# Attention scores: the second passes of the two maps on 64 rows each, in one encoder-layer kernel

## The chip, the cores and the metric

The kernel runs on one core of a Trainium2 chip. The metric is the device time of one execution in microseconds, the median of several runs. A core has a matrix engine (TensorE; in the profile PE for its matmuls, PEld for the loads of its stationary operand), VectorE (DVE), ScalarE (ACT), GpSimd (POOL) and SyncE (SP), which here only issues DMAs. TensorE reads two operands from on-chip memory (SBUF): a stationary one, loaded into the array first, whose partitions are the rows of the array and the dimension that is summed over, and a moving one, which streams through column by column. It writes to PSUM, which has eight banks of 512 fp32 columns.

## The reference, cut to what matters

One layer of an encoder works on 1,024 prompt frames and 64 frames of a running stream, model width 1,024. Beside a gated linear recurrence and a feed-forward part it has differential attention with 8 heads: each head has two score maps of width 64, and its weights are the difference of two softmaxes.

```python
def _diff_attend(q, k, v, lam, mask):
    """q [B,Q,H,2,d], k [B,S,H,2,d], v [B,S,H,2d], mask [Q,S] -> [B,Q,H,2d]."""
    s = jnp.einsum('bqhcd,bshcd->bhcqs', q.astype(jnp.float32), k.astype(jnp.float32)) * DA_SCALE
    s = jnp.where(mask, s, -jnp.inf)
    p = jax.nn.softmax(s, axis=-1)
    w = p[:, :, 0] - lam * p[:, :, 1]
    return jnp.einsum('bhqs,bshe->bqhe', w.astype(v.dtype), v)
```

For the prompt the mask is causal in chunks of 64 frames, so query tile i (128 frames, i from 0 to 7) looks at the first 128(i+1) keys. All of it is fp32.

## The kernel before

The stages follow one another: the recurrence with its projections, head by head; attention, head by head; the branch projections, normalisation, the up projection with a convolution, the down projection. Attention runs from about 640 to 1,345 us of the execution.

**fp32 out of fp32r.** A wide fp32 operand is split into a high part, rounded to the matmul type fp32r, and a low part, the remainder. A projection (`proj_chunk`, L178) sums three products in PSUM: high by high, high by low, low by high.

**The scores.** The scores use the array's 128 rows for two products at once, as a map is only 64 wide. For a head and 512 keys, tile `B` holds for map m on that map's own 64 rows (map 0 on rows 0 to 63, map 1 on 64 to 127) the high part of k, and on the other 64 rows the low part of k, which a DMA moves there. Tile `A` holds for 256 queries, two passes and two maps the part of q: pass 0 the high part, pass 1 the low part, made on the map's own 64 rows (VectorE L588, GpSimd L589) and copied by a DMA on SP's queue to the other 64 rows (L590). So pass 0 gives q-high by k-high plus q-high by k-low, pass 1 gives q-low by k-high plus q-low by k-low, both on 128 rows.

**A head's attention** (`da_attend`) goes through the query tiles from 7 down to 0. For tiles 7 to 4 (over 512 keys) each map has a PSUM tile `s` of two banks; for tiles 3 to 0 both maps share one such tile, a bank each. The pool has two of them. Per map: the score matmuls (L641), a masking write (L649 or L658), the row maximum (VectorE, L650 or L659), the exponential (ScalarE, L652 or L662), after which the buffer is free. Then the maps are combined on VectorE (L669), transposed on TensorE (L676), copied (ScalarE, L677) and multiplied with the values (L682). Tile 7's scores of the next head stand between the transposes of its values (`nat`, L330); `ckt` (L611), `yt` (L538) and `wtd` (L720) are other transposes; `wtd`, and `yt` once a head, are on 64 rows.

**What sets the order.** The program is written head by head; a scheduler with a simulated timeline then orders each engine's instructions when the program is built. It puts matmuls of the projections (L178) of the next head and of the gates between the steps of a head's attention. On the chip each engine works in that order.

Of the kernel before, what the change touches and what calls it, by code (L numbers as in the profile page):

```python
# [10 lines left out]
F32 = mybir.dt.float32  # L11
# [9 lines left out]
P = 128  # L21
# [29 lines left out]
class K:  # L51
# [489 lines left out]
    def da_prep(self, h, mm, dp):  # L541
        nc, a, o = self.nc, self.a, self.o
        w = a["w_in"][0]
        c = h * P
        V, S, G = nc.vector, nc.scalar, nc.gpsimd

        def ev(dst, scale=None):
            def f(c0, cw, ps):
                if scale is None:
                    S.copy(dst[:, c0:c0 + cw], ps)  # L550
                else:
                    S.mul(dst[:, c0:c0 + cw], ps, scale)
            return f

        def st(name, shape=(P, T)):
            return dp.tile(list(shape), F32, tag="st", name=f"{name}{h}", bufs=3)

        kT = st("kT")
        self.proj(mm, self.wcols(w, 5120 + c), self.x, ev(kT))
        B = []  # L560
        for hf in range(2):
            b = dp.tile([P, 2, 512], F32R, tag="B", name=self.nm("B"), bufs=4)
            kl = dp.tile([P, 512], F32R, tag="KL", name=self.nm("KL"), bufs=1)
            sl = slice(hf * 512, hf * 512 + 512)
            for m in range(2):
                r = slice(m * 64, m * 64 + 64)
                V.tensor_copy(b[r, m, :], kT[r, sl])  # L567
                G.tensor_tensor(kl[r], kT[r, sl], b[r, m, :].bitcast(F32), ALU.subtract)  # L568
                ro = slice(64 - m * 64, 128 - m * 64)
                nc.sync.dma_start(b[ro, m, :].bitcast(F32), kl[r].bitcast(F32))  # L570
            B.append(b)
        kd2 = dp.tile([P, 2, 64], F32R, tag="kd2", name=f"kd2{h}", bufs=2)
        V.tensor_copy(kd2[:, 0, :], kT[:, TP:])
        V.tensor_tensor(kd2[:, 1, :], kT[:, TP:], kd2[:, 0, :].bitcast(F32), ALU.subtract)
        kn = st("kn", (P, 9, P))
        self.to_natural(mm, kT, kn, "mm")
        nc.sync.dma_start(o["k_prompt"][0, 0, :, h, :].rearrange("(c p) e -> p c e", p=P), kn[:, 0:8, :])
        nc.sync.dma_start(o["k_sample"][0, 0, :, h, :], kn[:64, 8, :])
        qT = st("qT")
        self.proj(mm, self.wcols(w, 4096 + c), self.x, ev(qT, 0.125))  # L580
        A = [None] * 4
        for hf in (3, 2, 1, 0):
            t = dp.tile([P, 2, 2, 256], F32R, tag="A", name=self.nm("A"), bufs=5)
            sl = slice(hf * 256, hf * 256 + 256)
            for m in range(2):
                r = slice(m * 64, m * 64 + 64)
                ro = slice(64 - m * 64, 128 - m * 64)
                V.tensor_copy(t[r, 0, m, :], qT[r, sl])  # L588
                G.tensor_tensor(t[r, 1, m, :], qT[r, sl], t[r, 0, m, :].bitcast(F32), ALU.subtract)  # L589
                nc.sync.dma_start(t[ro, :, m, :].bitcast(F32), t[r, :, m, :].bitcast(F32))  # L590
            A[hf] = t
        qb = self.qbd[h % 2]
        for m in range(2):
            r = slice(m * 64, m * 64 + 64)
            V.tensor_copy(qb[r, 0, r], qT[r, TP:])
            V.tensor_tensor(qb[r, 1, r], qT[r, TP:], qb[r, 0, r].bitcast(F32), ALU.subtract)
        vT = st("vT")
        self.proj(mm, self.wcols(w, 6144 + c), self.x, ev(vT))
        vn = dp.tile([P, 9, P], F32, tag="vn", name=f"dvn{h}", bufs=2)
        self.to_natural(mm, vT, vn, "mm")  # L600
        nc.sync.dma_start(o["v_prompt"][0, 0, :, h, :].rearrange("(c p) e -> p c e", p=P), vn[:, 0:8, :])
        nc.sync.dma_start(o["v_sample"][0, 0, :, h, :], vn[:64, 8, :])
        ck = dp.tile([P, 8, P], F32, tag="ck", name=f"ck{h}", bufs=1)
        nc.sync.dma_start(ck, a["cache_k"][0, 0, :, h, :].rearrange("(c p) e -> p c e", p=P))
        cv = dp.tile([P, 8, P], F32, tag="cv", name=f"cv{h}", bufs=1)
        nc.sync.dma_start(cv, a["cache_v"][0, 0, :, h, :].rearrange("(c p) e -> p c e", p=P))
        kd = []
        for g in range(2):
            ps = mm.tile([P, 512], F32, tag="mm", name=self.nm("ckt"))
            for j in range(4):  # L610
                nc.tensor.transpose(ps[:, j * P:(j + 1) * P], ck[:, g * 4 + j, :], self.ident)  # L611
            t = dp.tile([P, 2, 512], F32R, tag="kd", name=self.nm("kd"), bufs=2)
            S.copy(t[:, 0, :], ps)
            V.tensor_tensor(t[:, 1, :], ps, t[:, 0, :].bitcast(F32), ALU.subtract)
            kd.append(t)
        kd.append(kd2)
        return A, B, vn, cv, kd, qb

    def da_attend(self, h, prep, sc, xs, avp, dp):
        nc, o = self.nc, self.o  # L620
        c = h * P
        V, S, G = nc.vector, nc.scalar, nc.gpsimd
        A, B, vn, cv, kd, qb = prep
# [5 lines left out]
        for i in range(7, -1, -1):  # L629
            n = (i + 1) * P  # L630
# [3 lines left out]
            s = dp.tile([P, 6], F32, tag="sm", name=self.nm("sm"), bufs=4)  # L634
            qc = slice((i % 2) * P, (i % 2) * P + P)

            def scores(dst, m):
                for kc in range((n + 511) // 512):
                    kw = min(512, n - kc * 512)
                    for p in range(2):  # L640
                        nc.tensor.matmul(dst[:, kc * 512:kc * 512 + kw], A[i // 2][:, p, m, qc],  # L641
                                         B[kc][:, m, :kw], start=(p == 0), stop=(p == 1))

            if n > 512:
                E = []
                for m in range(2):
                    ps = sc.tile([P, 1024], F32, tag="sc", name=self.nm("s"))
                    scores(ps, m)
                    V.memset(ps[0:64, n - 64:n], NEG)  # L649
                    V.tensor_reduce(s[:, m:m + 1], ps[:, :n], AX.X, ALU.max, negate=True)  # L650
                    e = dp.tile([P, 1024], F32, tag="E", name=self.nm("E"), bufs=4)
                    S.activation(e[:, :n], ps[:, :n], AF.Exp, bias=s[:, m:m + 1], accum_out=s[:, 2 + m:3 + m])  # L652
                    E.append(e[:, :n])
            else:
                ps = sc.tile([P, 2, 512], F32, tag="sc", name=self.nm("s"))
                for m in range(2):
                    scores(ps[:, m, :], m)
                V.memset(ps[0:64, :, n - 64:n], NEG)  # L658
                V.tensor_reduce(s[:, 0:2], ps[:, :, :n], AX.X, ALU.max, negate=True)  # L659
                e = dp.tile([P, 2, 512], F32, tag="E", name=self.nm("E"), bufs=4)  # L660
                for m in range(2):
                    S.activation(e[:, m, :n], ps[:, m, :n], AF.Exp, bias=s[:, m:m + 1],  # L662
                                 accum_out=s[:, 2 + m:3 + m])
                E = [e[:, 0, :n], e[:, 1, :n]]
# [6 lines left out]
            for g in range((i + 4) // 4):  # L671
                nb = min(4, i + 1 - g * 4)
                ps = xs.tile([P, 512], F32, tag="x", name=self.nm("wt"))
# [4 lines left out]
            for kb in range(i + 1):  # L678
                with ExitStack() as es:
                    if self.last_av is not None:  # L680
                        es.enter_context(self.tc.issue_after(self.last_av.ins))
                    self.last_av = nc.tensor.matmul(av[:, i % n4, :], wT[:, kb, :], vn[:, kb, :],  # L682
                                                    start=(kb == 0), stop=(kb == i))
# [544 lines left out]
```

## Time and profile before

| | |
|---|---|
| median of 3 runs (lowest to highest) | 2390.39 us (2389.98 to 2395.66) |
| the profiled execution's own time | 2388.49 us |
| its span, first to last instruction | 2386.6 us |
| mean granted TensorE clock | 0.995 |
| TensorE matmuls busy | 2337.9 us, 98% of the span |
| VectorE, ScalarE, GpSimd busy | 65%, 46%, 22% |
| score matmuls (L641) | 384, mean 354 ns |

The profile comes from one execution. A matmul's length is modelled: matmuls overlap in the array, so the pace is read from one start to the next, not from the length. A row of the timeline gives start and length in microseconds, engine, line, operation, the tiles written and read, rows times columns of the array and the shape that streams, and a count where equal instructions were merged. In brackets stands idle time of the engine ahead of it, and what ended it.

### The profile page before, as it was taken

To read this page: it belongs to the slowest core of one execution; us is meant where nothing else is said; L and a number is where in the kernel's file an instruction comes from. 1 tells how busy PE (TensorE), PEld (TensorE's weight loads), DVE (VectorE), ACT (ScalarE), POOL (GpSimd) and SP (SyncE) were. 2 spreads that over 40 slices of the span, in tenths; PEclk is the share of its full clock that TensorE was granted. 3 is DMA by queue.
4 is the path that set the end of the run, shared out by engine and by line. 5 is a ranking of instruction groups with operands and counts; after the bars stand their busy time and mean duration, and the time that the engine had idled before them with its cause. 6 is when DMAs were issued, how large, how long until landed. Compare 5 with 4: busy or idle time off the path is not lost.

```text
span 2386.6 us, 42975 instructions
## 1 busy us (share of the span) xinstructions
PE 2337.9 (98%) x16534; PEld 2283.0 (96%) x16534; DVE 1540.2 (65%) x2682; ACT 1103.7 (46%) x2134; POOL 520.7 (22%) x576
## 2 busy tenths in 40 slices
PE   8999999999999999999999999999999999999997
PEld 8999999999999999999999999999999999989997
DVE  3666665555566565655657565488977877766764
ACT  3444444443344434434436543257444444466664
POOL 2222222222621121120120000022544444200100
PEclk9999999999999999999999999999999999999999
DMA  4111111112622332332336684444323223298865
GB/s 129 40 40 47 40 47 47 42 31 66 202 79 84 94 86 81 95 92 75 102 90 199 183 260 139 134 144 144 113 87 95 82 86 95 85 275 251 245 200 150
DMA packets 404580, 273.02 MB, mean 114 GB/s; under 512 B 21803, under 2 KB 393927, under 8 KB 404374
## 3 DMA queue, kind: packets, MB, share of 16 engines
q1 hardware_dynamic: 399638, 265.52, 37.5%
q10 hardware_dynamic: 4224, 4.46, 0.5%
q8 instruction: 130, 2.13, 0.4%
q0 software_dynamic: 512, 0.29, 0.1%
q14 instruction: 76, 0.62, 0.1%
HBM read 199.65 MB, written 57.96 MB: 108 GB/s over the span
## 4 chain that ended last, share of the span: by engine, by line
PE 89%; DMA 3%; DVE 3%; ACT 2%; issue 1%; POOL 0%; SPq 0%; POOLq 0%; DVEq 0%; ACTq 0%
PE mm L178 47%; PE mm L151 17%; PE mm L1166 9%; PE s L641 3%; PE av L682 2%; PE wt L676 1%; PE lv L404 1%; PE nat L330 1%; DMA gb<-s_g 1%; PE o L487 1%; DMA ydl<-s_yd 1%; DMA wraw<-w_down 1%; PE o L490 1%; PE avd L727 1%; DVE wlo L83 1%
## 5 line engine op out<-in xcount | busy, mean ns | idle before, releaser
L178 PE MATMUL mm<-x,whi 128*128 128x362 f32 (+1 forms) x3456 | 876.4, 333 | 5.2 <-DMA wraw<-w_in 2.2
L178 PEld LDWEIGHTS mm<-x,whi 128*128 128x128 f32 x3456 | 611.8, 189 | 11.0 <-ACT x L308 4.7
L178 PE MATMUL mm<-x,wlo 128*128 128x362 f32 (+1 forms) x1728 | 573.1, 332 | 0.0
L83 DVE TENSOR_TENSOR wlo<-wraw,whi 128x512 fp32r<-128x512 f32 x516 | 364.7, 712 | 263.6 <-ACT whi L82 257.1
L82 ACT CAST whi<-wraw 128x512 fp32r<-128x512 f32 x516 | 309.0, 605 | 429.8 <-PE mm L178 203.8
L178 PEld LDWEIGHTS mm<-x,wlo 128*128 128x128 f32 x1728 | 326.5, 189 | 1.7 <-issue 1.0
L1166 PE MATMUL mm<-ah,whi 128*128 128x288 f32 (+1 forms) x688 | 200.3, 292 | 2.1 <-ACT ah L1150 2.1
L1166 PE MATMUL mm<-al,whi 128*128 128x288 f32 (+1 forms) x688 | 199.9, 291 | 1.5 <-DVE al L1151 1.5
L1166 PE MATMUL mm<-ah,wlo 128*128 128x288 f32 (+1 forms) x688 | 200.1, 292 | 0.1
L1166 PEld LDWEIGHTS mm<-ah,whi 128*128 128x128 f32 x688 | 131.1, 191 | 2.7 <-ACT ah L1150 2.4
L1166 PEld LDWEIGHTS mm<-al,whi 128*128 128x128 f32 x688 | 130.8, 190 | 1.9 <-DVE al L1151 1.9
L1166 PEld LDWEIGHTS mm<-ah,wlo 128*128 128x128 f32 x688 | 130.6, 190 | 0.8 <-DVE wlo L83 0.8
L532 POOL TENSOR_TENSOR rs<-rs,mhalf 128x4 f32<-128x4 f32 (+1 forms) x24 | 22.0, 917 | 373.4 <-DVE rs L531 373.4
L568 POOL TENSOR_TENSOR KL<-kT,B 64x512 fp32r<-64x512 f32 x32 | 49.3, 1539 | 218.1 <-DVE B L567 193.5
L641 PE MATMUL s<-B,A 128*128 128x512 f32 (+3 forms) x384 | 87.8, 354 | 2.3 <-ACT E L662 1.6
L82 ACT CAST whi<-wsum 128x512 fp32r<-128x512 f32 x80 | 49.5, 620 | 87.4 <-PE mm L151 83.8
L165 DVE TENSOR_TENSOR u<-mm,p 128x272 f32<-128x272 f32 (+2 forms) x160 | 55.1, 366 | 49.5 <-PE mm L151 49.5
L384 POOL TENSOR_TENSOR P<-X,k 128x544 f32<-128x544 f32 (+1 forms) x32 | 60.3, 1884 | 122.8 <-ACT X L378 76.3
L677 ACT COPY wT<-wt 128x512 f32<-128x512 f32 (+1 forms) x96 | 46.3, 482 | 80.1 <-PE wt L676 79.5
L1081 DVE SCALAR_TENSOR_TENSOR c<-u,par,c 128x1090 f32<-128x1090 f32 x44 | 80.6, 1831 | 0.9 <-ACT c L1078 0.9
L682 PE MATMUL av<-dvn,wT 128*128 128x128 f32 x576 | 80.0, 275 | 0.5 <-ACT wT L677 0.5
L99 POOL TENSOR_TENSOR wsum<-wraw,wraw 128x512 f32<-128x512 f32 x40 | 70.4, 1760 | 43.7 <-DVE wlo L83 43.5
(382 smaller groups left out, 5882.2 us busy)
## 6 DMA issues: line engine op xcount, KB each, us to landing
wraw<-w_down SPq DMA_DIRECT2D x160, 256.0 KB, 3.6
wraw<-w_in SPq DMA_DIRECT2D x144, 256.0 KB, 2.9
wraw<-w_up SPq DMA_DIRECT2D x124, 256.0 KB, 3.1
wraw<-w_br_hg SPq DMA_DIRECT2D x48, 256.0 KB, 4.0
s_act<-c SPq DMA_DIRECT2D x22, 512.0 KB, 3.0
A<-A SPq DMA_DIRECT2D x64, 128.0 KB, 2.5
wraw<-w_out SPq DMA_DIRECT2D x32, 256.0 KB, 3.0
araw<-s_act SPq DMA_DIRECT2D x44, 144.0 KB, 4.0
```

Of the source, the lines that this page charges most:

```text
L82: nc.scalar.copy(hi[:, :kn, :], raw[:, :kn, :])
L83: nc.vector.tensor_tensor(lo[:, :kn, :], raw[:, :kn, :], hi[:, :kn, :].bitcast(F32), ALU.subtract)
L99: G.tensor_tensor(t, x, y, op)
L151: nc.tensor.matmul(ps, l, r, start=(first and k == 0 and i == 0), stop=(k == 3 and i == 2), skip_group_check=not first)
L165: V.tensor_tensor(dst, ps[:, sl], d[other][:, sl], ALU.add)
L178: nc.tensor.matmul(ps[:, :cw], l, r[:, :cw], start=(k == 0 and i == 0), stop=(k == n - 1 and i == 2))
L384: G.tensor_tensor(pk, xv[:, :, :hb], blocks(k, B)[:, :, :hb], ALU.mult)
L568: G.tensor_tensor(kl[r], kT[r, sl], b[r, m, :].bitcast(F32), ALU.subtract)
L641: nc.tensor.matmul(dst[:, kc * 512:kc * 512 + kw], A[i // 2][:, p, m, qc], B[kc][:, m, :kw], start=(p == 0), stop=(p == 1))
L682: self.last_av = nc.tensor.matmul(av[:, i % n4, :], wT[:, kb, :], vn[:, kb, :], start=(kb == 0), stop=(kb == i))
L1081: V.scalar_tensor_tensor(t[:, :W - 2], u[:, i, 1:W - 1], par[:, self.o_w1 + j:self.o_w1 + j + 1], t[:, :W - 2], ALU.mult, ALU.add)
L1166: nc.tensor.matmul(ps[:, :cw], l, r[f][:, :cw], start=(f == 0 and i == 0), stop=(f == NF - 1 and i == 2))
```

## The change

For query tiles 2 to 7 the second pass takes only the map's own 64 rows: q-low by k-high. The product q-low by k-low is left out there. Map 0's second pass stands on rows 0 to 63, map 1's on rows 64 to 127, and both write to different banks. Tiles 1 and 0 keep 128 rows. The loops are turned round: pass outermost, then the 512 keys, then the map, and for tiles 7 to 4 both maps' PSUM tiles are taken before the scores are written. Since the low part of q is no longer needed on the other 64 rows for queries from 256 on, those copies carry the high part alone (three of the four `A` tiles of a head).

```diff
@@ da_prep
-                nc.sync.dma_start(t[ro, :, m, :].bitcast(F32), t[r, :, m, :].bitcast(F32))
+
+                parts = slice(0, 1 if hf else 2)
+                nc.sync.dma_start(t[ro, parts, m, :].bitcast(F32), t[r, parts, m, :].bitcast(F32))
@@ da_attend
-            def scores(dst, m):
-                for kc in range((n + 511) // 512):
-                    kw = min(512, n - kc * 512)
-                    for p in range(2):
-                        nc.tensor.matmul(dst[:, kc * 512:kc * 512 + kw], A[i // 2][:, p, m, qc],
-                                         B[kc][:, m, :kw], start=(p == 0), stop=(p == 1))
+            def scores(dsts):
+
+
+                spans = [(kc, min(512, n - kc * 512)) for kc in range((n + 511) // 512)]
+                halves = [slice(0, P)] * 2 if i < 2 else [slice(0, 64), slice(64, P)]
+                for p in range(2):
+                    for kc, kw in spans:
+                        for m in range(2):
+                            r = halves[m] if p else slice(0, P)
+                            nc.tensor.matmul(dsts[m][:, kc * 512:kc * 512 + kw], A[i // 2][r, p, m, qc],
+                                             B[kc][r, m, :kw], start=(p == 0), stop=(p == 1))
 
             if n > 512:
                 E = []
-                for m in range(2):
-                    ps = sc.tile([P, 1024], F32, tag="sc", name=self.nm("s"))
-                    scores(ps, m)
+                pss = [sc.tile([P, 1024], F32, tag="sc", name=self.nm("s")) for _ in range(2)]
+                scores(pss)
+                for m, ps in enumerate(pss):
                     V.memset(ps[0:64, n - 64:n], NEG)
...
             else:
                 ps = sc.tile([P, 2, 512], F32, tag="sc", name=self.nm("s"))
-                for m in range(2):
-                    scores(ps[:, m, :], m)
+                scores([ps[:, m, :] for m in range(2)])
```

The scheduler makes a new order of it. Its rows name the tile written, the moving and the stationary one, and the tile written's shape. On TensorE, in head 4, query tile 7 stood like this before (`s_1237` is map 0, `s_1239` map 1, `B_1198` and `B_1200` the first and second 512 keys; x2 are the two passes):

```order
L330 MATMUL nat_1227_9236<-ident_67,vT4_9144 128x128 x4
L641 MATMUL s_1237_9277<-B_1198_8984,A_1214_9112 128x512 x2
L641 MATMUL s_1237_9277<-B_1200_8992,A_1214_9112 128x512 x2
L641 MATMUL s_1239_9286<-B_1198_8984,A_1214_9112 128x512 x2
L641 MATMUL s_1239_9286<-B_1200_8992,A_1214_9112 128x512 x2
L538 MATMUL yt_1138_8583<-ident_67,rt_1135_8572 128x128 x4
```

And now (`s_1237` map 0, `s_1238` map 1):

```order
L330 MATMUL nat_1227_9236<-ident_67,vT4_9144 128x128 x4
L648 MATMUL s_1237_9277<-B_1198_8984,A_1214_9112 128x512
L648 MATMUL s_1238_9278<-B_1198_8984,A_1214_9112 128x512
L648 MATMUL s_1237_9277<-B_1200_8992,A_1214_9112 128x512
L648 MATMUL s_1238_9278<-B_1200_8992,A_1214_9112 128x512
L648 MATMUL s_1237_9277<-B_1198_8984,A_1214_9112 128x512
L648 MATMUL s_1238_9278<-B_1198_8984,A_1214_9112 128x512
L648 MATMUL s_1237_9277<-B_1200_8992,A_1214_9112 128x512
L648 MATMUL s_1238_9278<-B_1200_8992,A_1214_9112 128x512
L538 MATMUL yt_1138_8583<-ident_67,rt_1135_8572 128x128 x4
```

The first four are the first passes on 128 rows, the last four the second passes, by turns on rows 0 to 63 and 64 to 127.

The next query tile, 6, before, map 0 (`s_1245`) and, after 18 projection matmuls, map 1 (`s_1247`):

```order
L676 MATMUL wt_1150_8633<-ident_67,E_1148_8625 128x128 x3
L641 MATMUL s_1245_9321<-B_1198_8984,A_1214_9112 128x512 x2
L641 MATMUL s_1245_9321<-B_1200_8992,A_1214_9112 128x384 x2
L178 MATMUL mm_1319_9647<-x00_96,whi_1314_9637 128x364
...
L676 MATMUL wt_1155_8657<-ident_67,E_1153_8649 128x128 x2
L641 MATMUL s_1247_9330<-B_1198_8984,A_1214_9112 128x512 x2
L641 MATMUL s_1247_9330<-B_1200_8992,A_1214_9112 128x384 x2
```

And now (map 0 `s_1245`, map 1 `s_1246`), with the same 18 between:

```order
L682 MATMUL wt_1150_8633<-ident_67,E_1148_8625 128x128 x3
L648 MATMUL s_1245_9321<-B_1198_8984,A_1214_9112 128x512
L648 MATMUL s_1245_9321<-B_1200_8992,A_1214_9112 128x384
L648 MATMUL s_1245_9321<-B_1198_8984,A_1214_9112 128x512
L648 MATMUL s_1245_9321<-B_1200_8992,A_1214_9112 128x384
L178 MATMUL mm_1319_9647<-x00_96,whi_1314_9637 128x364
...
L682 MATMUL wt_1155_8657<-ident_67,E_1153_8649 128x128 x2
L648 MATMUL s_1246_9322<-B_1198_8984,A_1214_9112 128x512
L648 MATMUL s_1246_9322<-B_1200_8992,A_1214_9112 128x384
L648 MATMUL s_1246_9322<-B_1198_8984,A_1214_9112 128x512
L648 MATMUL s_1246_9322<-B_1200_8992,A_1214_9112 128x384
```

Here each map's two second passes follow its own first passes, and the two maps' second passes do not stand next to each other.

## The prediction

> **What bounds the kernel now.** I read the page's busy shares and chain first, then one window over the attention stage, then what TensorE waits for in it.
>
> ```profile
> PE 2337.9 (98%) x16534; PEld 2283.0 (96%) x16534; DVE 1540.2 (65%) x2682; ACT 1103.7 (46%) x2134; POOL 520.7 (22%) x576
> PE 89%; DMA 3%; DVE 3%; ACT 2%; issue 1%; POOL 0%; SPq 0%; POOLq 0%; DVEq 0%; ACTq 0%
> 640.00:1345.00 705.00, 695.30 (x4484) 665.61 (x4482) 429.89 (x929) 322.16 (x730) 112.31 (x115) 1.00 0.36 104
> PE mm L178 <- ACT whi L82: 2.4, 2, 1.5
> PE s L641 <- ACT E L662: 1.6, 1, 1.6
> PE wt L676 <- ACT yT L539: 1.2, 5, 0.2
> PE wtd L723 <- ACT wTd L721: 1.0, 1, 1.0
> PE mm L178 <- DVE t L937: 0.8, 1, 0.8
> PE s L641 <- ACT E L652: 0.6, 1, 0.6
> PE ckt L611 <- ACT dvn L331: 0.6, 1, 0.6
> PE mm L178 <- DVE kd L614: 0.5, 1, 0.5
> PE av L682 <- ACT wT L677: 0.5, 1, 0.5
> ```
>
> TensorE is 98% busy, 89% of the chain lies on it, and in the 705 us of attention (granted clock 1.00) its waits sum to 9.2 us (the nine rows). VectorE has 275 us to spare there, ScalarE 383. So what the change does to TensorE's own stream is what it does to the time, nearly one for one; no other engine can take it up.
>
> **The pace of the stream.** In the next rows, of the timeline (start, length, engine, line), a wide matmul starts as fast as its columns pass: two of 362 columns from 1251.34 to 1251.67, 0.166 us each; which is 0.45 to 0.46 ns a column. Four score matmuls with 1,792 columns take 0.90 from 992.86 to 993.76, 0.81 by that pace and 0.09 at their first weight load. I take 0.231 us for 512 columns and 0.174 for 384. A weight load follows the one before it by 0.11 (a pair takes 0.30, one 0.19) and hides behind the running matmul.
>
> ```profile
> 992.86 1.06 PE L641 MATMUL s<-B,A 128*128 128x512 f32 x4
> 993.76 0.50 PE L178 MATMUL mm<-x,whi 128*128 128x364 f32 x2
> ...
> 1251.34 0.50 PE L178 MATMUL mm<-x,whi 128*128 128x362 f32 x2
> 1251.67 0.32 PE L178 MATMUL mm<-x,wlo 128*128 128x362 f32 x1
> ...
> 1252.17 0.32 PE L178 MATMUL mm<-x,wlo 128*128 128x362 f32 x1
> 1252.42 0.27 PE L538 MATMUL yt<-ident,rt 64*128 64x64 f32 x1
> 1252.63 0.60 PE L178 MATMUL mm<-x,whi 128*128 128x362 f32 x2
> 1253.06 0.33 PE L178 MATMUL mm<-x,wlo 128*128 128x362 f32 x1
> ```
>
> **What a matmul on 64 rows costs its neighbours.** The kernel has such matmuls already; L538 above is one, on 64 of the array's 128 rows (64*128) between two wide ones. The weight loads at the same place:
>
> ```profile
> 1252.01 0.19 PEld L178 LDWEIGHTS mm<-x,wlo 128*128 128x128 f32 x1
> 1252.42 0.14 PEld L538 LDWEIGHTS yt<-ident,rt 64*128 64x128 f32 x1 [0.23 <-PE mm L178]
> 1252.62 0.30 PEld L178 LDWEIGHTS mm<-x,whi 128*128 128x128 f32 x2
> ```
>
> The load for L538 isn't hidden any more: it starts 0.07 before the modelled end of the wide matmul (1252.49), and so does the load for the next wide one before L538's end (1252.69). After a 512-column matmul it is the same (end 799.53, load 799.45):
>
> ```profile
> 798.21 1.32 PE L641 MATMUL s<-B,A 128*128 128x512 f32 x5
> 799.45 0.14 PEld L538 LDWEIGHTS yt<-ident,rt 64*128 64x128 f32 x1 [0.36 <-issue]
> ```
>
> So where the row size changes, the array runs empty before weights go in. The next data come 0.11 after the load, 0.04 after the modelled end, where unchanged they would come at the pace: after 362 columns 0.32 + 0.04 against 0.166, 0.20 us lost; after the 512-column one, whose last started at 799.13 (798.21 + 4 x 0.231), 799.56 against 799.36, 0.20; by the mean modelled lengths of the score matmuls (408 and 338 ns, rows below) 0.22 after 512 columns and 0.20 after 384. **A change costs 0.20 us**, upper bound 0.22. Lower bound: the whole detour by L538, 1252.17 to 1253.06, 0.89, against 0.61 for the same four at their pace (3 x 0.166 + 0.11): 0.28 for two changes, 0.14 each, where a short matmul has little to hide anyway.
>
> The type isn't what costs: between score matmuls (fp32r) and plain fp32 ones on 128 rows nothing is lost. Three score matmuls from 1269.97 should take 2 x 0.231 + 0.12 = 0.58, and L682 starts 0.59 later:
>
> ```profile
> 1269.97 0.75 PE L641 MATMUL s<-B,A 128*128 128x512 f32 x3
> 1270.56 0.60 PE L682 MATMUL av<-dvn,wT 128*128 128x128 f32 x4
> ...
> L641 PE MATMUL s<-B,A 128*128 128x512 f32 x192 | 57.8, 408 | 0.7 <-ACT E L652 0.6
> L641 PE MATMUL s<-B,A 128*128 128x384 f32 x64 | 15.1, 338 | 0.0
> ```
>
> **The change, part by part.** *Row-size changes added.* By the order of the changed program, only query tiles 7, 3 and 2 issue both maps' second passes next to each other. In tiles 6, 5 and 4 all of map 0 comes first, both passes, then projection matmuls, then all of map 1, since map 1's PSUM buffer is freed later. So a head has 1 + 3 x 2 + 1 + 1 = 9 excursions to 64 rows, 18 changes; eight heads make 144. A count over TensorE's whole order gives 252 changes of row size against 100 (in a few heads another matmul splits an excursion in two): **152 more, x 0.20 = 30.4 us** (21 at 0.14, 33 at 0.22).
>
> *Time saved.* A 64-row matmul streams as many columns as a 128-row one, so it saves only where its partner runs at once: two pairs of 512 in tile 7, one of 512 in tile 3, one of 384 in tile 2; 32 pairs of the 80. No row here shows two at once. Bounds: nothing, or a whole matmul per pair, 2 x 0.231 + 0.231 + 0.174 = 0.87 us a head, 6.9 in all. I take that the two weight loads go one after the other as all loads in the rows do, 0.11 apart: tile 7 saves 0.46 - 0.11 = 0.35, tile 3 0.12, tile 2 0.06, together **0.54 a head, 4.3 us**. In tiles 6 to 4 a second pass gains nothing.
>
> The Trainium skill, "TensorE: Matmul & The Clock Gate", Part 3, has matmuls of different row groups start about 4 ns apart; by that the pairs save nearly the upper 6.9 and the sum is 2.6 us lower, which no run here shows yet.
>
> *Waits.* In tile 7 both buffers must be complete before either is reduced, so map 0's VectorE reduction starts about 0.7 us later. From head 2 on this has cover: at head 4 the reduction ends at 984.64, but its exponential starts at 986.50, behind a copy (L677) that waits for other work, and tile 6's first matmul (987.90) comes after its end.
>
> ```profile
> 983.42 1.22 DVE L650 TENSOR_REDUCE sm<-s 128x1 f32<-128x1024 f32 x1
> 986.02 0.59 ACT L677 COPY wT<-wt 128x512 f32<-128x512 f32 x1
> 986.50 1.12 ACT L652 ACTIVATE E<-s,sm 128x1024 f32<-128x1024 f32 x1
> 987.90 1.06 PE L641 MATMUL s<-B,A 128*128 128x512 f32 x4
> ```
>
> In heads 0 and 1, where the exponential follows the reduction at once, I allow 0.7 us each, +1.4. Without the cover it would be 0.7 in all eight, 5.6. Against it, a slower TensorE swallows part of its 9.2 us of waits; I take 3. Queued behind a wait at tile 6's start are the projections, which only TensorE itself needs soon.
>
> *Copies.* 48 of the 64 copies of q's lower parts carry 64 KB instead of 128, on SP's queue, with DMA at 0.36 in this stage and no wait of TensorE for them in the nine rows: nothing.
>
> **Sum:** 30.4 - 4.3 + 1.4 - 3 = +24.5 us. Against the profiled execution's 2388.5 (span 2386.6) that is 2413; the runs' median lies 1.9 higher, so **2415 us**, 1.0% slower.
>
> **The rivals.**
> *A. Loads overlap too.* The pairs save 6.9: 2412. Against it: no load in the rows starts sooner than 0.11 after another. For it: those all load the same rows of the array.
> *B. Pairs don't overlap, or moving from the upper to the lower 64 rows empties the array like a change of size.* Without overlap 2419; with five such moves a head, 40 x 0.20 = 8 more, 2427. Also here: tile 7's wait without cover, +4. For it: nothing in the trace runs at once. The Trainium skill, "TensorEngine Tiling (Array Packing)", Key Properties, says a change of tiling mode drains the array and a change of tile doesn't; on the first the trace agrees with its 0.20 us, the second no run shows.
> *C. The waits swallow more,* all 9.2 us: 2409, or 2405 with short-matmul prices at part of the changes.
> *D. Not slower.* The price belongs to the plain fp32 and transpose matmuls, which are all that runs on 64 rows now; fp32r loads would be fetched early as usual. Then only the gain is left: 2384 to 2386, within 0.3%. It decides if a change costs under 0.03 to 0.05 us (4.3 or 6.9 over 152). Against it: the wide loads on the way back (1252.62) are fp32r and wait just the same.
>
> **How the numbers follow.** About 0.3% is what a measurement of this kernel can tell from no change. Forecast 0.55, A 0.20, B 0.12, C 0.08, D 0.05. Range: 2405 (C) to 2425 (most of B) leaves out D, and B's far end. Slower by over 0.3% holds for all but D and a little of C: 0.93; within it 0.05; faster by more needs D with the whole overlap and some luck: 0.02.
>
> **What would show it.** Score rows with 64*128; before each group of them, and after, a weight load 0.07 before the last matmul's modelled end, with idle time put down to issue or to the matmul before. Tile 7's partners starting 0.11 apart (A: next to nothing; B: a full 0.23 or more); tiles 6 to 4 with second passes 0.23 apart, as now. The attention stage longer by some 25 us, and the rest as long as before. I am wrong if weight loads on 64 rows start while a 128-row matmul streams, or if the stages outside attention move by more than 3 us.

## The result and the profile after

The changed kernel takes 2407.85 us (median of 6 runs, 2404.6 to 2411.07) beside 2392.35 for the kernel before (6 runs): a ratio of 1.0062, 95% interval 1.0049 to 1.0075, 0.6% slower. In a second measurement, beside the later experiments, the ratio was 1.0078 (1.0064 to 1.0093). The forecast was 2415, 1.0% slower, with a range of 2405 to 2425. The profiled execution took 2404.6 us, its span 2402.8, 16.2 more than before.

The page of the changed kernel, its engines and its chain:

```profile
PE 2352.1 (98%) x16534; PEld 2269.2 (94%) x16534; DVE 1536.3 (64%) x2682; ACT 1104.2 (46%) x2134; POOL 521.5 (22%) x576
PE 88%; DMA 4%; DVE 3%; ACT 2%; issue 2%; POOL 0%; SPq 0%; POOLq 0%; ACTq 0%; DVEq 0%
```

In its windows, attention (which ends 16 us later, at the same work) and what follows it; behind the stretch and its length stands the busy time of each engine, PE first and PEld next:

```profile
640.00:1361.00 721.00, 712.73 (x4475) 654.75 (x4473) 424.75 (x925) 321.96 (x730) 111.36 (x114) 1.00 0.33 97
1361.00:2402.00 1041.00, 1018.12 (x7939) 1012.32 (x7939) 741.73 (x1237) 510.78 (x1026) 235.53 (x341) 0.99 0.51 154
```

What TensorE waits for in attention (total us, number, longest):

```profile
PE wtd L729 <- ACT wTd L727: 1.2, 1, 1.2
PE s L648 <- ACT E L668: 1.2, 1, 1.2
PE wt L682 <- ACT yT L539: 1.2, 5, 0.2
PE s L648 <- ACT E L659: 1.0, 2, 0.7
PE mm L178 <- ACT whi L82: 0.6, 1, 0.6
PE ckt L613 <- ACT dvn L331: 0.6, 1, 0.6
PE mm L178 <- DVE kd L616: 0.5, 1, 0.5
PE mm L178 <- DVE t L943: 0.4, 1, 0.4
```

The rest of the program takes 1041 us as before, to about a microsecond; the 16 us lie in attention. Matmuls count as busy 17 us longer there, though as many columns are streamed: their lengths are modelled and overlap less where the starts lie further apart. Weight loads are busy 11 us less. TensorE's waits fell from 9.2 to 6.7 us, so it isn't waiting that got longer. What did shows in the weight loads by shape (the last columns: idle time ahead of them and what ended it), the changed kernel's second passes first, then all its other score loads:

```profile
L648 PEld LDWEIGHTS s<-B,A 64*128 64x128 f32 x160 | 19.8, 184 | 20.2 <-issue 19.7 <-POOL A L589 0.4
L648 PEld LDWEIGHTS s<-B,A 128*128 128x128 f32 x224 | 35.1, 189 | 5.6 <-issue 2.0 <-ACT E L659 1.5 <-ACT E L668 1.5
```

20 us in which the load path stands still ahead of a 64-row load and nothing in the profile is waited for ("issue").

**Tile 6's map 0 in head 4**, the timeline of the changed kernel (start, length, engine, line): matmuls, then loads:

```profile
995.92 1.26 PE L648 MATMUL s<-B,A 128*128 128x512 f32 x4
997.11 0.60 PE L178 MATMUL mm<-x,whi 128*128 128x364 f32 x2
...
995.89 0.30 PEld L648 LDWEIGHTS s<-B,A 128*128 128x128 f32 x2
996.50 0.29 PEld L648 LDWEIGHTS s<-B,A 64*128 64x128 f32 x2 [0.31 <-issue]
997.11 0.30 PEld L178 LDWEIGHTS mm<-x,whi 128*128 128x128 f32 x2 [0.31 <-DVE kd L616]
```

From the first score matmul to the data of the next projection (its load at 997.11 plus 0.11) are 1.30 us; before, such a four took 0.90 where nothing was waited for (map 1's, 992.86 to 993.76). The excursion costs 0.40, 0.20 a change. At this place not all of it is new time: in the kernel before, the load behind map 0's four came 1.06 after their first start (987.90), as it waited for VectorE:

```profile
988.96 0.30 PEld L178 LDWEIGHTS mm<-x,whi 128*128 128x128 f32 x2 [0.33 <-DVE kd L614]
```

In the changed kernel the load at 997.11 is put down to VectorE too, but that result was there at 996.93. So 1.30 stands against 1.17 here (988.96 + 0.11), and 0.27 of the 0.40 falls into time that was waited before. Over the whole trace, from the start of the last matmul ahead to the second one behind, the excursions of tiles 6 and 5 cost 0.395 to 0.40 against the same matmuls at their pace.

**Tile 7 in head 4**, the same two views:

```profile
990.13 1.84 PE L648 MATMUL s<-B,A 128*128 128x512 f32 x8
991.91 0.66 PE L538 MATMUL yt<-ident,rt 128*128 128x128 f32 x4
...
990.11 0.77 PEld L648 LDWEIGHTS s<-B,A 128*128 128x128 f32 x4
991.24 0.30 PEld L648 LDWEIGHTS s<-B,A 64*128 64x128 f32 x4 [0.37 <-issue]
991.91 0.42 PEld L538 LDWEIGHTS yt<-ident,rt 128*128 128x128 f32 x4 [0.37 <-issue]
```

Four 64-row loads take 0.30, as long as two on 128 rows: each pair's loads and matmuls start together (3 to 4 ns apart in the trace, one pair of matmuls 6). The Trainium skill, "TensorE: Matmul & The Clock Gate", Part 3, gives about 4 ns between matmuls of different row groups; the trace agrees. The eight score matmuls and the load behind them end at 992.02 (991.91 + 0.11), 1.89 after the first; before it was 1.94 (982.01 to 983.95, rows of the kernel before):

```profile
982.01 2.10 PE L641 MATMUL s<-B,A 128*128 128x512 f32 x8
983.95 0.60 PE L538 MATMUL yt<-ident,rt 128*128 128x128 f32 x4
```

So two pairs just pay for an excursion; by the whole trace four 64-row matmuls with both changes take 0.11 less than four at their pace. Tile 3, with one pair of 512, loses 0.17, tile 2 0.22.

**Tile 4**, whose last score matmul ahead of a change has 128 columns, loses less:

```profile
1013.47 0.94 PE L648 MATMUL s<-B,A 128*128 128x512 f32 x4
1014.34 0.44 PE L178 MATMUL mm<-x,wlo 128*128 128x362 f32 x1
1014.61 0.49 PE L178 MATMUL mm<-x,whi 128*128 128x362 f32 x2
```

0.97 from 1013.47 to 1014.44 against 2 x (0.231 + 0.11) = 0.68: 0.29, or 0.15 a change. It isn't the 128 columns alone: where a plain fp32 matmul of 128 columns (L682, L688) stands ahead of an excursion, the trace has 0.395 to 0.40 as elsewhere. All score excursions of the trace together cost 21.6 us against the same matmuls one after the other.

### The profile page after: what moved, and what is told of

Read it like the earlier page. It is cut to its first block, busy times and chain, and to the rows that moved or that the text cites. A ratio compares the mean times of both kernels' runs of the same rounds, so it can differ in the third digit from the quotient of the medians.

```text
span 2402.8 us, 42971 instructions
## 1 busy us (share of the span) xinstructions
PE 2352.1 (98%) x16534; PEld 2269.2 (94%) x16534; DVE 1536.3 (64%) x2682; ACT 1104.2 (46%) x2134; POOL 521.5 (22%) x576
## 4 chain that ended last, share of the span: by engine, by line
PE 88%; DMA 4%; DVE 3%; ACT 2%; issue 2%; POOL 0%; SPq 0%; POOLq 0%; ACTq 0%; DVEq 0%
PE mm L178 46%; PE mm L151 17%; PE mm L1172 9%; PE s L648 3%; PE av L688 2%; PE wt L682 1%; PE lv L404 1%; PE nat L330 1%; DMA gb<-s_g 1%; PE o L487 1%; DVE wlo L83 1%; DMA ydl<-s_yd 1%; PE o L490 1%; DMA wraw<-w_down 1%; PE avd L733 1%
## 5 line engine op out<-in xcount | busy, mean ns | idle before, releaser
L648 PE MATMUL s<-B,A 64*128 64x512 f32 (+7 forms) x384 | 95.6, 379 | 2.2 <-ACT E L668 1.2
L688 PE MATMUL av<-dvn,wT 128*128 128x128 f32 x576 | 80.7, 276 | 0.1
```

The costliest lines, as they stand in the source:

```text
L648: nc.tensor.matmul(dsts[m][:, kc * 512:kc * 512 + kw], A[i // 2][r, p, m, qc], B[kc][r, m, :kw], start=(p == 0), stop=(p == 1))
```

## The experiments

Theory 1: time is lost where the array changes between 64 and 128 rows, and pairs overlap because they use different rows. Its rivals: the loops' turn makes TensorE wait for both buffers; a 64-row matmul has a price of its own; the overlap has nothing to do with the rows. The first four runs were made to give a different number under each.

**The new order, all on 128 rows.**

```diff
-                halves = [slice(0, P)] * 2 if i < 2 else [slice(0, 64), slice(64, P)]
+                halves = [slice(0, P)] * 2
-                parts = slice(0, 1 if hf else 2)
+                parts = slice(0, 2)
```

> The changed loops and both PSUM buffers taken first, as in the change, but every second pass on 128 rows (and the copies whole again); 100 changes of row size, as in the kernel before. Theory 1 (what costs is the change between 64 and 128 rows): the time of before, 2392, within 4 us. Rival (what costs is that a tile's scores need both buffers, so that TensorE waits): most of the 15.5 us stay, 2403 to 2408.

Measured: 2392.75 us beside 2390.56, ratio 1.0008 (0.9998 to 1.0017). The order and the buffers are worth 2.2 us by the medians, 4 at most by the interval, where the waiting rival needs 11 to 16. It falls. The trace shows still less: heads 4 to 6 stand 91.04 us apart, 91.02 in the kernel before.

**64 rows in the old order.**

```diff
+                        r = slice(m * 64, m * 64 + 64) if p and i > 1 else slice(0, P)
-                        nc.tensor.matmul(dst[:, kc * 512:kc * 512 + kw], A[i // 2][:, p, m, qc],
-                                         B[kc][:, m, :kw], start=(p == 0), stop=(p == 1))
+                        nc.tensor.matmul(dst[:, kc * 512:kc * 512 + kw], A[i // 2][r, p, m, qc],
+                                         B[kc][r, m, :kw], start=(p == 0), stop=(p == 1))
```

> The loops and buffers of before, only the second passes of tiles 2 to 7 on the map's own 64 rows; q-low by k-low is left out there. Each second pass is now an excursion of its own: 418 changes of row size, 318 more than before, and no two second passes next to each other. Theory 1: 159 excursions of 0.40 us (0.29 after 128 columns) are 61 us, less some 5 that waits swallow: 2392 + 56 = 2448, from 2440 to 2455. Rival (a 64-row matmul has a price of its own, and there are 160 of them here as in the change): the change's 15.5 plus the 6.9 that its pairs save, 2415.

Measured: 2447.17, ratio 1.0231 (1.0212 to 1.0249), 56.6 us by the medians. With twice the added changes (318 against 152) and no pair it loses over three times as much, as theory 1 has it; the per-matmul rival (2415) falls. Its tile 7 in head 4, matmuls and then the first loads:

```profile
1013.67 3.48 PE L642 MATMUL s<-B,A 128*128 128x512 f32 x8
1017.07 0.44 PE L538 MATMUL yt<-ident,rt 128*128 128x128 f32 x2
...
1014.07 0.18 PEld L642 LDWEIGHTS s<-B,A 64*128 64x128 f32 x1 [0.24 <-issue]
1014.49 0.19 PEld L642 LDWEIGHTS s<-B,A 128*128 128x128 f32 x1 [0.24 <-issue]
1014.92 0.18 PEld L642 LDWEIGHTS s<-B,A 64*128 64x128 f32 x1 [0.25 <-issue]
```

Every load comes 0.24 after the end of the one before, alone, at 64 and at 128 rows. The eight matmuls take 3.51 us (to 1017.07 + 0.11) against 1.94: 0.39 for each of four excursions.

**Pairs in every tile** (second passes held behind both maps' first passes).

```diff
-                            nc.tensor.matmul(dsts[m][:, kc * 512:kc * 512 + kw], A[i // 2][r, p, m, qc],
-                                             B[kc][r, m, :kw], start=(p == 0), stop=(p == 1))
+                            with ExitStack() as es:
+                                if p and i > 1:
+                                    es.enter_context(self.tc.issue_after(last.ins))
+                                last = nc.tensor.matmul(dsts[m][:, kc * 512:kc * 512 + kw], A[i // 2][r, p, m, qc],
+                                                        B[kc][r, m, :kw], start=(p == 0), stop=(p == 1))
```

> The change, with the second passes of a tile held in program order behind the first passes of both maps, so that tiles 6, 5 and 4 have pairs too (q-low by k-low left out as in the change). 198 changes of row size, 98 more than before, instead of 152 more. Theory 1: an excursion costs 0.40 (0.29 after 128 columns) and a pair gives back a whole matmul: tile 7 -0.1, 6 0.0, 5 +0.06, 4 -0.04, 3 +0.17, 2 +0.22, together 0.3 us a head, 2.4 in all, and up to 5 for waits on the second buffer: 2392 to 2399. Rival (waits for both buffers are the cost): it must get worse than the change, since tiles 6 to 4 now wait for both: 2410 to 2420.

Measured: 2394.78, ratio 1.0013 (1.0002 to 1.0024): 0.1% slower than before, where the change is 0.6 to 0.8% slower. All 80 pairs start together now. Tile 6, where map 1's first passes and now all four second passes stand together:

```profile
996.76 1.26 PE L651 MATMUL s<-B,A 128*128 128x512 f32 x6
997.95 0.60 PE L178 MATMUL mm<-x,whi 128*128 128x364 f32 x2
```

Six matmuls take 1.30 us (to 997.95 + 0.11), as long as four in the change. Of its waits, one row is the price of holding the second passes back:

```profile
PE mm L178 <- DVE kd L616: 3.4, 8, 0.5
```

3.4 us in eight pieces (0.5 in the change): the projection behind map 0's first passes, with only those two matmuls ahead of it, waits for VectorE. So most of the loss came from the scheduler's pulling the maps apart, and even with all pairs together the idea only breaks even.

**Both maps on the same rows.**

```diff
-                halves = [slice(0, P)] * 2 if i < 2 else [slice(0, 64), slice(64, P)]
+                halves = [slice(0, P)] * 2 if i < 2 else [slice(0, 64)] * 2
-                parts = slice(0, 1 if hf else 2)
+                parts = slice(0, 2)
```

> The change with both maps' second passes on rows 0 to 63 (for map 1 this multiplies q-low by k-low instead of q-low by k-high, so its second pass is another product; the copies are whole again). Order and number of row-size changes as in the change, 252. Theory 1 with pairs that overlap because they use different rows: the 32 pairs run one after the other, 6.9 us more than the change, 2413 to 2417. Rival (the pairs' overlap in the trace is only how starts are recorded, or any two 64-row matmuls overlap): the time of the change, 2406 to 2410.

Measured: 2415.18, ratio 1.0097 (1.0077 to 1.0116) to before, 7.3 us above the change's first median and 4.2 above its second: in the direction of theory 1, but between measurements made at different times. The trace is clearer:

```profile
996.96 2.30 PE L648 MATMUL s<-B,A 128*128 128x512 f32 x8
999.20 0.44 PE L538 MATMUL yt<-ident,rt 128*128 128x128 f32 x2
...
998.07 0.75 PEld L648 LDWEIGHTS s<-B,A 64*128 64x128 f32 x4 [0.37 <-issue]
```

Four loads take 0.75 instead of 0.30, and tile 7 2.35 us instead of 1.89: two matmuls' time more. Heads 4 to 6 repeat every 94.39 us instead of 93.57, 6.6 for eight. The overlap needs different rows.

**Tile 7 alone on 64 rows.**

```diff
-                halves = [slice(0, P)] * 2 if i < 2 else [slice(0, 64), slice(64, P)]
+                halves = [slice(0, P)] * 2 if i < 7 else [slice(0, 64), slice(64, P)]
-                parts = slice(0, 1 if hf else 2)
+                parts = slice(0, 2)
```

> The change for query tile 7 alone (q-low by k-low left out there only); tiles 6 to 0 keep 128 rows. 14 more changes of row size than before, and 16 of the 80 pairs, the only ones that save more than their excursion costs: in the trace of the changed kernel four 64-row matmuls with both changes took 0.11 us less than four on 128 rows. Theory 1: 8 x 0.11 = 0.9 us less, up to 1.5 more for the later reduction in heads 0 and 1: the time of before within 3 us. Rival (part of the 15.5 us comes from tile 7, whose reduction starts later): 3 to 6 us more than before.

Measured: 2390.84 beside 2393.08, ratio 0.9994 (0.9984 to 1.0004). By its time, the one part of the change with a gain on paper can't be told from no change. The trace has the gain: heads 4 to 6 stand 90.91 us apart instead of 91.02, the 0.11 expected.

**The kernel before with whole rows elsewhere.** If a change of size costs TensorE time anywhere, the kernel before pays for 290 of them. The core of this edit:

```diff
@@ to_natural (L330), the last 64 frames
-                nc.tensor.transpose(ps[:m, i * P:(i + 1) * P], src[:, c * P:c * P + m], self.ident)
+                nc.tensor.transpose(ps[:, :P], src[:, T - P:T], self.ident)
+                nc.scalar.copy(dst[:TS, 8, :], ps[TS:P, :P])
@@ hgrn (L463, L487), rows 64 to 127 of kn, vn zeroed
-        nc.tensor.matmul(U2[:, :P], kn[:64, 8, :], vn[:64, 8, :], start=True, stop=True)
+        nc.tensor.matmul(U2[:, :P], kn[:, 8, :], vn[:, 8, :], start=True, stop=True)
-                intra = (vn[:m, ch, :], att[:m, ch, :m])
+                intra = (vn[:, ch, :], att[:, ch, :m])
@@ rms_out (L538), the rest of tf zeroed
-            nc.tensor.transpose(ps[:, i * m:(i + 1) * m], t[:, i, :], self.ident[:m, :m])
+            nc.tensor.transpose(ps[:, i * P:(i + 1) * P], tf[:, i, :], self.ident)
@@ decode (L723, L728), the rest of E2w, wT, vn zeroed
-        nc.tensor.transpose(ps[:64, :64], E2[:64, :], self.ident[:64, :64])
+        nc.tensor.transpose(ps[:, :P], E2w, self.ident)
-        nc.tensor.matmul(av[:64, :P], wT[:64, 8, :], vn[:64, 8, :], start=False, stop=True)
+        nc.tensor.matmul(av[:64, :P], wT[:, 8, :], vn[:, 8, :], start=False, stop=True)
```

> The kernel before, scores unchanged, but small matmuls elsewhere filled up with zeros or with neighbouring columns so that they use the array in its full size: the last transposes of each head (L330, L538, L723) and the products with the 64 sample frames (L463, L487, L728). 170 changes of tile size instead of 290 (20 of row size instead of 100, and 40 fewer of column size), for some GpSimd writes of zeros. Theory 1, if the price holds for every change of size: 120 x 0.14 to 0.20 is 17 to 24 us, some of it taken back by waits: 2368 to 2378. Rival (only the wide score matmuls pay it, short transposes hide it): 2386 to 2391. Second rival (changes of column size cost nothing): 80 x 0.14, 2378 to 2382.

Measured: 2383.82 beside 2393.08, ratio 0.9965 (0.9953 to 0.9976): 8 us faster than before (5.7 to 11.2 by the interval), and faster than either kernel of this case. The place of L538 (here L547), matmuls and loads:

```profile
1069.30 0.33 PE L178 MATMUL mm<-x,wlo 128*128 128x362 f32 x1
1069.47 0.27 PE L547 MATMUL yt<-ident,rt 128*128 128x128 f32 x1
1069.50 0.58 PE L178 MATMUL mm<-x,whi 128*128 128x362 f32 x2
1069.91 0.33 PE L178 MATMUL mm<-x,wlo 128*128 128x362 f32 x1
...
1069.31 0.14 PEld L547 LDWEIGHTS yt<-ident,rt 128*128 128x128 f32 x1
1069.47 0.30 PEld L178 LDWEIGHTS mm<-x,whi 128*128 128x128 f32 x2
```

The detour that took 0.89 us takes 0.61. But I expected 17 to 24 us in all, and the result lies between the two rivals; the interval touches both. Loads by shape in the kernel before show why it is less:

```profile
L727 PEld LDWEIGHTS avd<-cv,wTd 128*64 128x64 f32 x128 | 13.8, 137 | 1.8 <-issue 1.8
L463 PEld LDWEIGHTS U<-vn,kn 64*128 64x128 f32 x16 | 2.4, 185 | 1.9 <-issue 1.9
L330 PEld LDWEIGHTS nat<-ident,vT 128*64 128x64 f32 x16 | 1.8, 111 | 0.0
```

The load path idles ahead of a 64-row product (L463) and of a 64-column product (L727), but not ahead of a 64-column transpose (L330). The way back from L330 is free too: around the one at 690.28 us, from the matmul ahead to the second one behind are 0.33, three times 0.11. Of the 120 changes that I took away, 40 were of column size alone, at L330, and cost nothing that shows. Eighty at 0.14 are 11.2 us, the interval's upper end, and the spacing of the heads bears the second rival out: 90.38 us instead of 91.02 in attention, 67.12 instead of 67.80 in the recurrence, together 1.32 a head, 10.6 for eight, within the interval.

**The change once more.**

> The changed kernel once more, beside the others of this call: 1.006 to 1.007 of before.

Measured: 2410.97 beside 2393.08, ratio 1.0078 (1.0064 to 1.0093), above what was expected; over both measurements the loss is between 0.5 and 0.9%. Heads 4 to 6 stand 93.56 us apart in this profile, as in the first (93.57).

## Why the prediction was right, and where its sizes were off

- **TensorE's own stream decides: right.** Its waits fell while the stage grew, nothing outside moved, and the new order alone did nothing.
- **The price of a change, 0.20 us: right for 256, 384 and 512 columns, too high for tile 4.** There 16 excursions cost 0.29 instead of 0.40, 1.7 us less. The prediction had this lower bound from L538's short detour and still put 0.20 on all 152.
- **Time saved by pairs, 4.3 us: mis-sized, it is 6.9.** This was rival A. The step that failed is "the two weight loads go one after the other": the rows that it was read from all load the same rows of the array. Rival A's own counter to them was the right reading, and the run with both maps on the same rows brings the 0.23 spacing back.
- With these two, 30.4 - 1.7 - 6.9 = 21.8, and the trace's own sum is 21.6.
- **Waits, +1.4 - 3: mis-sized.** The delayed reduction cost 0.4, not 1.4: TensorE's waits for L659 are 1.0 us against 0.6 before. From the first score matmul to the last branch projection the two profiles differ by 18.0 us (778.06 against 760.03), so 3.6 of the 21.6 were swallowed there, net, where the prediction had 1.6; the waits named in the rows fell by 2.5. The other 1.8 down to the span's 16.2 lie outside and have nothing to do with the change: 0.7 in the first 27 us of the execution, and 1.1 behind the branch projections, mostly in one place. There, between 1412.8 and 1416.0 us, the kernel before starts its 272-column matmuls 0.23 us apart instead of 0.12 to 0.13: its granted clock was 0.83 from 1410 to 1420 us, while the changed kernel had 1.00 at the same work (1427 to 1437). That is 1.6 us of luck in the changed kernel's favour, and half a us of later start against it. Heads that seldom wait show the price: tile 7 of head 5 in the changed kernel, after 990.13 in head 4, and below it in the kernel before, after 982.01:

```profile
1083.71 1.61 PE L648 MATMUL s<-B,A 128*128 128x512 f32 x6
```

```profile
1073.03 1.18 PE L641 MATMUL s<-B,A 128*128 128x512 f32 x4
```

By these rows the heads stand 93.58 and 91.02 us apart: 2.56 a head, 20.5 for eight. By the trace the excursions of one such head sum to 2.86; 0.27 of the difference is the load behind tile 6's map 0, which waited before. The first heads and the last gave more back.

- **Tiles 6 to 4 get no pairs: right,** as the order told; holding them together took most of the loss away (0.6 to 0.8% became 0.1%).
- **The copies, nothing:** made whole again together with 128-row passes they change nothing that stands clear of the noise.
- **Rivals.** A was right on the loads. B falls: pairs overlap, and there is no gap between the two halves, as tile 7's four loads in 0.30 show. The Trainium skill, "TensorEngine Tiling (Array Packing)", Key Properties, has only a change of tiling mode drain the array, not a change of tile; these four loads agree. D falls: fp32r loads on 64 rows wait like the others. C's mechanism, waits that swallow part, was there with 3.6 us where it had 9.2.
- **Luck.** The price, the pairs, the waits and the stretches outside attention all missed to the same side, so the result lies near the low end of the range, in the first measurement closest to C's 2409. That it is C's figure is chance: C had it from waits alone.

## What to carry to other kernels

Count a matmul's price in a dense stream with its neighbours: two wide pairs on half the rows saved what the way there and back cost, so by these prices such packing pays only if more pairs stand together, and a scheduler that doesn't know the price may pull them apart; read the order of the built program before counting the gain. Look then for small matmuls already there: filling them up to the full array gave 0.35%. And when a row shows that two things don't overlap, ask whether they used the same part of the hardware.

## What was not expected of the hardware

- Loads on different halves of the rows run at once: four in 0.30 us, four on the same rows in 0.75.
- 64-column transposes (L330) leave no gap (0.0 us idle ahead of 16 loads), 64-column products (L727, 1.8 us ahead of its 128 loads) and 64-row transposes (L538, 0.23 at 1252.42) do.
- The granted clock falls for a few microseconds in some executions and not in others. The seventh head of the recurrence, long before attention, takes 68.2 us in four of the nine profiled executions and 70.6 to 71.3 in the other five, of the changed kernel too (68.24 in the first profile, 71.32 in the second). From 548 to 565 us the granted clock was 1.00 in the four and 0.80 in the five. The spread between runs goes the same way: of the 19 runs of the kernel before beside the last experiments, the two with a mean clock of 0.996 took 2385.9 and 2386.1 us, the two with 0.992 2393.6 and 2394.4. Why the clock falls where it does was not looked for.
